# Reciprocal square roots of the norms as one GpSimd power instruction, in a two-block transformer kernel on one core

## The chip, the cores and the metric

The kernel runs on one core of a Trainium2 chip. The metric is the device time of one execution in microseconds (us). Engine names are those of the profile: PE is TensorE's matmul, PEld its weight load, DVE is VectorE, ACT is ScalarE, POOL is GpSimd, SP is SyncE, which here only issues DMAs.

## The reference

Two different transformer blocks of two layers each run one after the other on 256 tokens of width 1024, in float32. Every sublayer is wrapped in RMS norms, and the heads of the second block have norms of their own:

```python
def rmsnorm(x, g):
    y = x * lax.rsqrt(jnp.mean(x * x, -1, keepdims=True) + EPS)      # EPS = 1e-6
    return y * g

# first block, layer 0: gated delta rule and mLSTM; layer 1: windowed attention
h = h + rmsnorm(mix, gains[1])
hn = rmsnorm(h, gains[2])
ff = jnp.square(jax.nn.relu(hn @ w_up[layer])) @ w_down[layer]
h = h + rmsnorm(ff, gains[3])
h = h + jax.nn.sigmoid(h @ w_ple_gate[layer]) * (p[layer] @ w_ple[layer])

# second block, each layer: five groups of four heads (latent attention, forgetting attention, block
# attention, differential attention, memory attention), with norms over each head of q and k
xn = rmsnorm(x, attn_norm[l]);  x = x + concat(five groups of xn @ w_in[l]) @ w_o[l]
xn = rmsnorm(x, ffn_norm[l]);   x = x + (silu(conv(xn @ w_gate)) * (xn @ w_up)) @ w_down
```

## The kernel before, in words

Tokens lie on the 128 partitions in two token tiles, `t = 0` and `t = 1`, so that a norm of a row of 1024 is one column `[128, 1]` for each token tile, and the head norms of one tile are 3 to 16 columns. Weights come in blocks of 1 MB into two `raw` buffers; ACT (or DVE) rounds each into a high part `hi`, DVE takes the rest as a low part `lo`, and every product is three matmuls (high by high, low by high, high by low). The transposed activations stand in `aTh` and `aTl`. All instructions are written down by a `Recorder`, which then puts them into an order of its own: each engine gets, of what can start first, the instruction with the longest way to go, by rough prices in ns (`price`) and latencies between engines (`LAG`). All instructions are issued from one line (L571), so the profile is read by tiles: `s` are small tiles of up to 32 columns (the norms' scalars), `w` work tiles, `ps` PSUM banks, `gb` gains, `h` the residual stream.

A reciprocal square root is `rsqrt_of`: a guess from the bits on DVE (an int32 instruction), then a cubic and a quadratic step. For one column these are six further instructions, each of which goes to POOL or DVE (`rec.scalar`), whichever the planner finds free; for several columns they are ten instructions on POOL. The users are:

- `normed_T` (start of the program and, through `to_ff2`, ahead of each feed-forward of the second block): the row's factor is needed before the rows are transposed, so that PE waits for it.
- `residual` in `pre_ff1` and in `post` (first block): `h += y * r`, and the next transposes wait for `h`.
- `scaled_T`: the transposes take the rows without their factor; `r[t]` is multiplied in later, when banks are read.
- `headnorm`, `foxqk`, `group0` and `differential` in `mixers2` (second block): DVE multiplies the heads by their factors, and most of these products read a PSUM bank, which is free only then.
- `delta_out` (first block's layer 0), two columns each.

Where an input went in without its row's factor `r`, the norm that follows multiplies `r` in: `rsq(ms, w, r)` and `residual(..., pre)` work out `r * (r*r*ms + EPS) ** -0.5`.

Of the kernel before, what the change touches and what calls it, by code (L numbers as in the profile page):

```python
# [10 lines left out]
F32 = mybir.dt.float32  # L11
# [25 lines left out]
# ---------------------------------------------------------------- layout of small inputs  # L37
# [35 lines left out]
# ---------------------------------------------------------------- constants of the shapes  # L73
# [66 lines left out]
def layout(x):  # L140
# [126 lines left out]
class Recorder:  # L267
    """Takes the program's instructions down in the order in which it names them, and issues them in another:
    each engine gets, of what can start first, the instruction with the longest way to go. Every order of two
    instructions on overlapping data is kept, and a pool's tile is taken ahead of its turn only if the  # L270
    program's own order still fits into the pool from there on."""
# [12 lines left out]
    # ---------------------------------------------------------------- taking down  # L284
# [24 lines left out]
    def copy(self, out, src, scale=1.0):  # L309
        """out = scale * src on ScalarE or VectorE"""  # L310
# [67 lines left out]
    def price(self, op, out, ins):  # L378
        """a rough time in ns"""
# [66 lines left out]
    def swap(self, op):  # L446
        """the other form of an instruction"""
# [6 lines left out]
    def arrange(self):  # L454
# [33 lines left out]
        p0, gone, out = 0, [False] * n, []  # L488
        by_rank, top = sorted(range(n), key=lambda i: -ops[i].rank), 0
        while len(out) < n:  # L490
# [4 lines left out]
            for e, cand in avail.items():  # L495
                pick = None
                for i in cand:
# [9 lines left out]
                    for t in op.tiles:  # L507
                        if t not in taken:
                            p = pool[t]
                            room = self.pools[p] - (KEEP.get(p, 0) if op.rank < lead - SLACKTIME else 0)  # L510
                            if first[t] > p0 and use[p][p0 : first[t]].max() >= room:
# [62 lines left out]
class Loom:  # L574
    """Chains of dependent steps, each taken as far as what it needs is there."""
# [36 lines left out]
    def until(self, ready, *keys):  # L612
        """within a chain: wait for keys in ready"""
# [5 lines left out]
def program(ctx, tc, A, out, dbg=None):  # L619
# [64 lines left out]
    # ------------------------------------------------------------ resident data  # L684
# [51 lines left out]
    def whole(name, i, k, w):  # L736
        """block i of a packed weight as it is, for float32 products: four passes, but nothing to prepare"""
# [22 lines left out]
    def nmm(banks, a, hi, lo, first, last, n=512):  # L760
        """banks (column halves of n) += act^T @ W for one k-tile"""
# [1320 lines left out]
```

## Time and profile before

| | before |
|---|---|
| median of 3 runs | 1451.15 us (1449.95 to 1454.01) |
| span of the profiled execution, first to last instruction | 1450.2 us |
| TensorE busy | 1401.3 us |
| GpSimd busy | 199.9 us, 607 instructions |
| VectorE busy | 1000.2 us, 2320 instructions |

The profiled execution is known by its span alone; the median of the runs stands 0.9 us above it. Busy is the time in which an engine worked on at least one instruction.

### The profile page before, as it was taken

The page shows a single profiled execution, that of the slowest core. Times are in us where ns is not written, and L with a number is a line of the kernel's source. Part 1 is how long each engine was busy: PE and PEld are TensorE (multiplying, and loading weights), DVE is VectorE, ACT ScalarE, POOL GpSimd, SP SyncE. Part 2 cuts the span into 40 slices and gives each one's busy share as a digit, 9 for nine tenths or more (in the row PEclk, how much of TensorE's full clock was granted, in tenths as well). Part 3 has the DMA queues.
Part 4 walks back from the last instruction along what each step waited for, and adds up shares of the span by engine and source line. Part 5 has one row for each costly group of instructions (what it writes and reads, how often), then busy time and mean ns, then how long its engine had stood idle before and what let it go on. Part 6 is the DMA issues. An engine that isn't in the chain of part 4 may idle for free.

```text
span 1450.2 us, 23721 instructions
## 1 busy us (share of the span) xinstructions
PE 1401.3 (97%) x8856; PEld 1239.8 (85%) x8868; DVE 1000.2 (69%) x2320; ACT 796.1 (55%) x1810; POOL 199.9 (14%) x607
## 2 busy tenths in 40 slices
PE   7999999999999989999998999999999999999998
PEld 6899879999788879998786788999997778799997
DVE  6986776555778666556888766676567685656664
ACT  5554555444556635445575875564447586455543
POOL 0000530000110130000136412000004631100000
PEclk9999999999999999999999999999999999999999
DMA  8521344554553444545454222555544421345553
GB/s 331 190 88 59 116 172 166 209 193 177 208 191 126 158 160 166 212 175 213 146 206 170 108 103 88 204 203 180 198 157 174 149 103 59 118 166 182 184 196 115
DMA packets 36116, 236.40 MB, mean 163 GB/s; under 512 B 4128, under 2 KB 4384, under 8 KB 9888
## 3 DMA queue, kind: packets, MB, share of 16 engines
q1 hardware_dynamic: 36000, 234.88, 44.6%
q8 instruction: 70, 1.15, 0.3%
q14 instruction: 46, 0.38, 0.1%
HBM read 233.81 MB, written 1.05 MB: 162 GB/s over the span
## 4 chain that ended last, share of the span: by engine, by line
PE 76%; DVE 9%; POOL 9%; ACT 4%; issue 2%; DMA 0%; ACTq 0%; POOLq 0%; DVEq 0%
PE ps L571 76%; POOL s L571 9%; ACT w L571 3%; DVE w L571 3%; DVE s L571 2%; DVE lo L571 2%; DVE h L571 1%; DVE aTl L571 0%; DMA h<-in_x 0%; ACT hi L571 0%; ACT L571 0%; DVE tab L571 0%; ACT aTh L571 0%; ACT s L571 0%; DVE hi L571 0%
## 5 line engine op out<-in xcount | busy, mean ns | idle before, releaser
L571 ACT ACTIVATE hi<-raw 128x512 fp32r<-128x512 f32 (+1 forms) x789 | 436.7, 622 | 289.2 <-PE ps L571 241.6
L571 DVE TENSOR_TENSOR lo<-raw,hi 128x512 fp32r<-128x512 f32 (+2 forms) x836 | 522.2, 679 | 86.6 <-ACT hi L571 79.5
L571 PE MATMUL ps<-hi,w 128*128 128x512 f32 (+1 forms) x1272 | 390.6, 401 | 0.8 <-ACT w L571 0.6
L571 PE MATMUL ps<-aTh,hi 128*128 128x256 f32 x1256 | 327.6, 281 | 0.2 <-ACT aTh L571 0.2
L571 PE MATMUL ps<-aTh,lo 128*128 128x256 f32 x1256 | 323.7, 281 | 1.3 <-DVE lo L571 1.3
L571 PE MATMUL ps<-aTl,hi 128*128 128x256 f32 x1256 | 323.8, 281 | 0.7 <-DVE aTl L571 0.7
L571 PEld LDWEIGHTS ps<-hi,w 128*128 128x128 f32 x1272 | 222.0, 188 | 35.5 <-issue 1.9
L571 PEld LDWEIGHTS ps<-aTh,hi 128*128 128x128 f32 x1256 | 229.3, 189 | 11.1 <-ACT aTh L571 1.1
L571 PEld LDWEIGHTS ps<-aTh,lo 128*128 128x128 f32 x1256 | 227.7, 189 | 10.5 <-DVE lo L571 1.5
L571 PEld LDWEIGHTS ps<-aTl,hi 128*128 128x128 f32 x1256 | 226.9, 189 | 8.7 <-DVE aTl L571 1.0
L571 ACT ACTIVATE w<-ps 128x512 f32<-128x512 f32 (+4 forms) x260 | 131.3, 536 | 139.8 <-PE ps L571 133.4
L571 PE MATMUL ps<-lo,w 128*128 128x512 f32 (+1 forms) x620 | 202.6, 394 | 0.0
L571 PE MATMUL ps<-hi,aTh 128*128 128x512 f32 (+2 forms) x480 | 164.1, 373 | 4.1 <-DVE w L571 3.0
L571 PE MATMUL ps<-lo,aTh 128*128 128x512 f32 (+2 forms) x480 | 163.2, 370 | 4.9 <-DVE lo L571 4.9
L571 PE MATMUL ps<-hi,aTl 128*128 128x512 f32 (+2 forms) x480 | 162.8, 370 | 0.4 <-DVE aTl L571 0.3
L571 PE MATMUL ps<-w,w 128*128 128x128 f32 (+5 forms) x992 | 156.0, 286 | 1.3 <-DVE w L571 0.6
L571 POOL TENSOR_SCALAR s<-s 128x1 f32<-128x1 f32 (+6 forms) x222 | 78.2, 353 | 551.7 <-DVE s L571 294.0
L571 PEld LDWEIGHTS ps<-w,w 128*128 128x128 f32 (+1 forms) x992 | 139.2, 191 | 14.5 <-ACT w L571 2.7
L571 PE MATMUL ps<-cf,w 128*128 128x128 f32 (+1 forms) x612 | 115.3, 285 | 28.4 <-DVE w L571 23.6
L571 ACT ACTIVATE w<-w 128x512 fp32r<-128x512 f32 (+5 forms) x146 | 77.4, 538 | 109.4 <-DVE w L571 106.8
L571 PEld LDWEIGHTS ps<-cf,w 128*128 128x128 f32 (+1 forms) x612 | 81.8, 150 | 50.4 <-issue 18.5
L571 DVE CAST hi<-raw 128x512 fp32r<-128x512 f32 (+1 forms) x47 | 20.0, 425 | 151.5 <-PE ps L571 151.5
(101 smaller groups left out, 1348.6 us busy)
## 6 DMA issues: line engine op xcount, KB each, us to landing
raw<-in_wu SPq DMA_DIRECT2D x32, 1024.0 KB, 4.8
raw<-in_wd SPq DMA_DIRECT2D x32, 1024.0 KB, 5.4
raw<-in_fg SPq DMA_DIRECT2D x22, 1024.0 KB, 4.8
raw<-in_fu SPq DMA_DIRECT2D x22, 1024.0 KB, 4.8
raw<-in_fd SPq DMA_DIRECT2D x22, 1024.0 KB, 4.9
raw<-in_wi SPq DMA_DIRECT2D x20, 1024.0 KB, 4.8
raw<-in_w0t SPq DMA_DIRECT2D x10, 1024.0 KB, 4.8
raw<-in_wo SPq DMA_DIRECT2D x10, 1024.0 KB, 4.8
```

Source lines behind the costliest of these rows:

```text
L571: getattr(self.engines[op.eng], op.call)(*op.args, **op.kwargs)
```

## The change

Each reciprocal square root is one GpSimd instruction, `tensor_tensor` with the power operation and a constant tile of -0.5 (`root`). The rescaling by `RS` is gone with the polynomial; it remains in `rsqrt_rows`, the former polynomial on DVE, which one norm of 256 columns still uses. Where rows went in without their factor, the factor is no longer multiplied in: since `r = x ** -0.5`, `r * (r*r*ms + EPS) ** -0.5` equals `(ms + EPS * x) ** -0.5`, so the row brings its own eps (`row_eps`; after the squared feed-forward `EPS * x * x`). In `pre_ff1` the factor itself is then not needed at all, and no root is taken there. The planner has a price for the power, 300 ns and 165 ns for each column. Its search has a cache (`crowded`) that gives the same answers. Comments and docstrings are blanked, so that line numbers shift (L571 is L593).

```diff
         if op.eng == "pool":
+            if op.kwargs.get("op") == OP.pow:
+                return 300 + 165 * n
...
-    def rsqrt_of(x, w, eng, buf=None):
-        new = (lambda: small(w)[: x.shape[0]]) if buf is None else (lambda: buf()[: x.shape[0], :w])
-        z, t, q, xn = new(), new(), new(), new()
-        scalar = rec.scalar if w == 1 else eng.tensor_scalar
         dve.tensor_scalar(z.bitcast(I32), x.bitcast(I32), -0.5, 1597463007.0, op0=OP.mult, op1=OP.add)
-        scalar(xn, x, -1.0, None, op0=OP.mult)
...
+    nhalf = cpool.tile([P, 16], F32, name="nhalf")
+    pool.memset(nhalf, -0.5)
...
+    def root(x, w=1):
+        o = small(w)
+        pool.tensor_tensor(o, x, nhalf[:, :w], op=OP.pow)
+        return o
+
+    def rsq(ms, w=1, eps=None):
         x = small(w)
-        if r is None:
-            dve.tensor_scalar(x, ms, RS, RS * EPS, op0=OP.mult, op1=OP.add)
-            return rsqrt_of(x, w, pool)
-        r2 = small(1)
-        rec.scalar(r2, r, r, RS, op0=OP.mult, op1=OP.mult)
-        dve.tensor_scalar(x, ms, r2, RS * EPS, op0=OP.mult, op1=OP.add)
-        o = small(w)
-        rec.scalar(o, rsqrt_of(x, w, pool), r, None, op0=OP.mult)
-        return o
+        rec.scalar(x, ms, EPS if eps is None else eps, None, op0=OP.add)
+        return root(x, w)
...
+    def rms(srcs, both=True):
         a, b = meansq(srcs, D)
         x = small(1)
-        rec.scalar(x, a, b, RS * EPS, op0=OP.add, op1=OP.add)
-        return rsqrt_of(x, 1, pool)
+        rec.scalar(x, a, b, EPS, op0=OP.add, op1=OP.add)
+        return root(x) if both else None, x
+
+    def row_eps(x, n=1):
+        e = small(1)
+        if n == 1:
+            rec.scalar(e, x, EPS, None, op0=OP.mult)
+        else:
+            rec.scalar(e, x, x, EPS, op0=OP.mult, op1=OP.mult)
+        return e
...
-    def residual(t, banks, g, pre=None):
+    def residual(t, banks, g, eps=EPS):
...
-        if pre is None:
-            rec.scalar(x, a, b, RS * EPS, op0=OP.add, op1=OP.add)
-            r = rsqrt_of(x, 1, pool)
-        else:
-            p2, s, r = small(1), small(1), small(1)
-            rec.scalar(p2, pre, pre, None, op0=OP.mult)
-            rec.scalar(s, a, b, p2, op0=OP.add, op1=OP.mult)
-            rec.scalar(x, s, RS * EPS, None, op0=OP.add)
-            rec.scalar(r, rsqrt_of(x, 1, pool), pre, None, op0=OP.mult)
+        rec.scalar(x, a, b, eps, op0=OP.add, op1=OP.add)
+        r = root(x)
...
-        yield from scaled_T(t, g2, r)
+        yield from scaled_T(t, g2, None, e, 2)
...
-            residual(t, down[t], g3, pre=r2)
+            residual(t, down[t], g3, e[t])
...
-            headnorm(fold(bank, 8), y, 8, 64, r[t])
+            headnorm(fold(bank, 8), y, 8, 64, e[t])
```

The change leaves POOL 140 rows of 612 (counting constants and branches), among them 64 powers: 24 of one column, 8 of two, 4 of three, 12 of four, 8 of eight, 4 of twelve and 4 of sixteen. DVE has 2154 instructions instead of 2322. The SP queue has the same DMAs, with three neighbouring ones exchanged. All of this changes the planner's order; here are the places on which most rests.

On POOL, among the head norms of the second block's first layer, these rows work out one root of 16 columns (`s_1632` is the mean square with eps, `s_1635` the root; the rows of 12 columns belong to another). Before:

```order
L571 TENSOR_SCALAR s_1638<-s_1632 128x16
L571 TENSOR_TENSOR s_1593<-s_1599,s_1593 128x12
L571 TENSOR_TENSOR s_1636<-s_1635 128x16
L571 TENSOR_TENSOR s_1636<-s_1636,s_1632 128x16
L571 TENSOR_SCALAR s_1639<-s_1636 128x16
L571 TENSOR_TENSOR s_1637<-s_1639,s_1636 128x16
L571 TENSOR_SCALAR s_1640<-s_1637 128x16
L571 TENSOR_TENSOR s_1635<-s_1640,s_1635 128x16
L571 TENSOR_TENSOR s_1636<-s_1635 128x16
L571 TENSOR_TENSOR s_1636<-s_1636,s_1638 128x16
L571 TENSOR_SCALAR s_1641<-s_1636 128x16
L571 TENSOR_TENSOR s_1635<-s_1641,s_1635 128x16
```

Now, at the same place (`s_1277` and `s_1289` are the rows' eps):

```order
L593 TENSOR_SCALAR s_1441<-s_1438 128x12
L593 TENSOR_TENSOR s_1442<-s_1441,nhalf 128x12
L593 TENSOR_SCALAR s_1475<-s_1474,s_1277 128x16
L593 TENSOR_TENSOR s_1476<-s_1475,nhalf 128x16
L593 TENSOR_SCALAR s_1504<-s_1503,s_1289 128x16
L593 TENSOR_TENSOR s_1505<-s_1504,nhalf 128x16
```

Eleven dependent rows for each root have become two, an addition and the power.

On DVE, the start of the program (`h_81` and `h_82` are the token tiles, `s_90` and `s_102` their factors, `gb_85` the gain). Before:

```order
L571 TENSOR_SCALAR s_91<-s_90,s_93 128x1
L571 TENSOR_SCALAR s_101<-s_98 128x1
L571 TENSOR_SCALAR s_90<-s_91,s_90 128x1
L571 TENSOR_SCALAR s_102<-s_101 128x1
L571 TENSOR_SCALAR s_105<-s_101 128x1
L571 SCALAR_TENSOR_TENSOR w_94<-h_81,s_90,gb_85 128x512
L571 SCALAR_TENSOR_TENSOR w_95<-h_81,s_90,gb_85 128x512
L571 TENSOR_SCALAR s_103<-s_102,s_105 128x1
L571 TENSOR_SCALAR s_102<-s_103,s_102 128x1
L571 SCALAR_TENSOR_TENSOR w_106<-h_82,s_102,gb_85 128x512
L571 SCALAR_TENSOR_TENSOR w_107<-h_82,s_102,gb_85 128x512
```

Now:

```order
L593 TENSOR_SCALAR s_90<-s_87 128x1
L593 TENSOR_SCALAR s_99<-s_96 128x1
L593 SCALAR_TENSOR_TENSOR w_92<-h_81,s_91,gb_86 128x512
L593 SCALAR_TENSOR_TENSOR w_93<-h_81,s_91,gb_86 128x512
L593 SCALAR_TENSOR_TENSOR w_101<-h_82,s_100,gb_86 128x512
L593 SCALAR_TENSOR_TENSOR w_102<-h_82,s_100,gb_86 128x512
```

Both tiles' products now follow each other with nothing between them.

On DVE, `pre_ff1` of the first block's second layer, where rows with `gb` and `ps` are the second tile's bias and those with `w` and `gb` the gain. Before:

```order
L571 TENSOR_TENSOR w_1113<-ps_1075,gb_1086 128x512
L571 TENSOR_TENSOR w_1114<-ps_1076,gb_1086 128x512
L571 TENSOR_TENSOR w_1118<-w_1113,gb_1087 128x512
L571 TENSOR_TENSOR w_1119<-w_1114,gb_1087 128x512
L571 SCALAR_TENSOR_TENSOR h_81<-w_1094,s_1097,h_81 128x512
L571 TENSOR_SCALAR s_1121<-s_1120 128x1
L571 SCALAR_TENSOR_TENSOR h_81<-w_1095,s_1097,h_81 128x512
L571 TENSOR_SCALAR s_1123<-s_1122 128x1
L571 TENSOR_TENSOR w_1101<-h_81,gb_1088 128x512
L571 TENSOR_SCALAR s_1122<-s_1121,s_1124 128x1
L571 TENSOR_TENSOR w_1102<-h_81,gb_1088 128x512
```

Now:

```order
L593 TENSOR_TENSOR w_1022<-ps_990,gb_1001 128x512
L593 SCALAR_TENSOR_TENSOR h_81<-w_1009,s_1012,h_81 128x512
L593 TENSOR_TENSOR w_1023<-ps_991,gb_1001 128x512
L593 TENSOR_TENSOR w_1027<-w_1022,gb_1002 128x512
L593 TENSOR_TENSOR w_1013<-h_81,gb_1003 128x512
L593 SCALAR_TENSOR_TENSOR h_81<-w_1010,s_1012,h_81 128x512
L593 TENSOR_TENSOR w_1028<-w_1023,gb_1002 128x512
L593 SCALAR_TENSOR_TENSOR h_82<-w_1027,s_1030,h_82 128x512
L593 TENSOR_TENSOR w_1014<-h_81,gb_1003 128x512
```

The small steps are gone, and the first tile's row for the transposes (`w_1013`, before `w_1101`) stands four wide rows after the second tile's first bias instead of six.

## Rows read from the trace of the kernel before

**Rows 1.** The page, span and busy times: us (share of the span) and instructions.

```profile
span 1450.2 us, 23721 instructions
PE 1401.3 (97%) x8856; PEld 1239.8 (85%) x8868; DVE 1000.2 (69%) x2320; ACT 796.1 (55%) x1810; POOL 199.9 (14%) x607
```

**Rows 2.** The page, chain that ended last: share of the span by engine.

```profile
PE 76%; DVE 9%; POOL 9%; ACT 4%; issue 2%; DMA 0%; ACTq 0%; POOLq 0%; DVEq 0%
```

**Rows 3.** Stretches at norms: length, busy PE, PEld, DVE, ACT, POOL, clock, DMA share.

```profile
150.00:200.00 50.00, 49.32 (x241) 39.45 (x241) 37.16 (x105) 25.88 (x63) 28.38 (x88) 1.00 0.39 137
...
196.00:206.00 10.00, 9.03 (x36) 5.19 (x35) 8.86 (x21) 8.68 (x21) 4.33 (x10) 1.00 0.34 124
386.00:397.00 11.00, 10.16 (x40) 5.94 (x38) 9.40 (x23) 7.74 (x17) 5.92 (x10) 1.00 0.37 127
...
700.00:708.00 8.00, 5.74 (x36) 4.21 (x34) 7.51 (x16) 7.55 (x17) 2.19 (x6) 1.00 0.19 67
741.00:818.00 77.00, 69.29 (x321) 55.15 (x320) 60.47 (x212) 49.28 (x109) 47.24 (x158) 0.98 0.46 166
...
893.00:903.00 10.00, 9.21 (x52) 7.34 (x52) 8.71 (x18) 8.11 (x18) 4.78 (x10) 1.00 0.29 107
1104.00:1180.00 76.00, 67.88 (x323) 54.58 (x324) 56.74 (x187) 50.90 (x116) 43.23 (x161) 0.98 0.47 166
```

**Rows 4.** PE in order of time, the longest gaps: idle before in brackets.

```profile
516.13 2.13 PE L571 MATMUL ps<-cf,w 128*128 128x128 f32 x8 [5.99 <-DVE w L571]
...
793.57 0.79 PE L571 MATMUL ps<-lo,aTh 128*128 128x512 f32 x1 [2.65 <-DVE lo L571]
...
1144.38 0.41 PE L571 MATMUL ps<-cf,w 128*128 128x128 f32 x2 [2.77 <-DVE s L571]
...
1256.73 0.63 PE L571 MATMUL ps<-cf,w 128*128 128x128 f32 x4 [2.61 <-DVE w L571]
```

**Rows 5.** The five us behind those gaps, columns as in rows 3.

```profile
516.00:521.00 5.00, 4.73 (x22) 4.00 (x22) 4.67 (x9) 2.99 (x7) 2.94 (x6) 0.55 0.04 15
...
793.00:798.00 5.00, 4.43 (x15) 3.54 (x16) 4.12 (x12) 1.47 (x3) 2.52 (x8) 0.66 0.32 92
1144.00:1149.00 5.00, 4.62 (x18) 3.70 (x19) 4.45 (x23) 1.67 (x4) 2.54 (x10) 0.66 0.24 102
...
1256.00:1261.00 5.00, 3.79 (x17) 3.16 (x18) 4.36 (x10) 2.95 (x6) 2.64 (x5) 0.67 0.00 0
```

**Rows 6.** DVE's waits for POOL, at 741 to 818 and at 1104 to 1180: us, times, longest.

```profile
DVE w L571 <- POOL s L571: 10.4, 9, 2.4
...
DVE w L571 <- POOL s L571: 8.6, 6, 2.7
```

**Rows 7.** POOL's instructions by form: busy us, mean ns, idle before.

```profile
L571 POOL TENSOR_SCALAR s<-s,s 128x1 f32<-128x1 f32 x69 | 37.6, 546 | 449.3 <-DVE s L571 278.0 <-ACT w L571 167.6 <-ACT hi L571 0.7
...
L571 POOL TENSOR_TENSOR s<-s,s 128x4 f32<-128x4 f32 x60 | 14.5, 246 | 4.1
...
L571 POOL TENSOR_TENSOR s<-s,s 128x16 f32<-128x16 f32 x20 | 6.5, 325 | 1.2
```

**Rows 8.** Small tiles, DVE and POOL: ns shortest/median/longest, first and last start.

```profile
L571 DVE TENSOR_SCALAR s<-s x192: 135/163/216, 5.4 to 1257.9; 128x2 f32<-128x2 f32 x44, 128x1 f32<-128x1 f32 x42, 128x1 int32<-128x1 int32 x28, 128x4 f32<-128x4 f32 x24
...
L571 POOL TENSOR_TENSOR s<-s,s x200: 191/203/2006, 149.9 to 1221.6; 128x4 f32<-128x4 f32 x27, 128x8 f32<-128x8 f32 x21, 128x2 f32<-128x2 f32 x20, 128x16 f32<-128x16 f32 x12
```

**Rows 9.** The start, in order of time: start us, us, instruction.

```profile
5.42 0.46 DVE L571 TENSOR_SCALAR s<-s 128x1 f32<-128x1 f32 x3 [5.42 <-ACT w L571]
...
7.36 1.34 POOL L571 TENSOR_SCALAR s<-s,s 128x1 f32<-128x1 f32 x1 [5.43 <-DVE s L571]
...
10.02 1.42 DVE L571 SCALAR_TENSOR_TENSOR w<-h,s,gb 128x512 f32<-128x512 f32 x2
```

**Rows 10.** Before the second feed-forward, in order of time, columns as in rows 9.

```profile
1254.20 0.68 DVE L571 TENSOR_TENSOR h<-ps,h 128x512 f32<-128x512 f32 x1
...
1259.63 1.41 DVE L571 SCALAR_TENSOR_TENSOR w<-h,s,gb 128x512 f32<-128x512 f32 x2
```

More of the change, by code (lines that the diff above doesn't have):

```diff
@@ L488, in arrange, with crowded, moved @@
         p0, gone, out = 0, [False] * n, []
+        full = {}
+        def crowded(p, room):
+            k = full.get((p, room))
+            if k is None or k < p0:
+                v = use[p][p0:n] >= room
+                k = p0 + int(v.argmax())
+                if k < n and not v[k - p0]:
+                    k = n
+                full[p, room] = k
+            return k
+        def moved(p):
+            room = self.pools[p]
+            full.pop((p, room), None)
+            full.pop((p, room - KEEP.get(p, 0)), None)
         by_rank, top = sorted(range(n), key=lambda i: -ops[i].rank), 0
@@ L510, in arrange @@
                             room = self.pools[p] - (KEEP.get(p, 0) if op.rank < lead - SLACKTIME else 0)
-                            if first[t] > p0 and use[p][p0 : first[t]].max() >= room:
+                            if first[t] > p0 and crowded(p, room) < first[t]:
                                 ok = False
@@ L545, in arrange @@
                 p = pool[t]
+                if t not in taken or left[t] == 1:
+                    moved(p)
                 if t not in taken:
@@ L808, in program, with rsqrt_rows @@
     RS = 4.0 * (8.0 / 3.0) ** 6
-    def rsqrt_of(x, w, eng, buf=None):
-        new = (lambda: small(w)[: x.shape[0]]) if buf is None else (lambda: buf()[: x.shape[0], :w])
-        z, t, q, xn = new(), new(), new(), new()
-        scalar = rec.scalar if w == 1 else eng.tensor_scalar
+    def rsqrt_rows(x, w, buf):
+        z, t, q, xn = (buf()[: x.shape[0], :w] for _ in range(4))
         dve.tensor_scalar(z.bitcast(I32), x.bitcast(I32), -0.5, 1597463007.0, op0=OP.mult, op1=OP.add)
-        scalar(xn, x, -1.0, None, op0=OP.mult)
+        dve.tensor_scalar(xn, x, -1.0, None, op0=OP.mult)
@@ L900, in scaled_T @@
             to_aT(t, q, xs[q])
-        r[t] = rms(halves(h[t]))
+        rr, x = rms(halves(h[t]), r is not None)
+        if r is not None:
+            r[t] = rr
+        if e is not None:
+            e[t] = row_eps(x, n)
     def normed_T(t, g):
-        r = rms(halves(h[t]))
+        r, _ = rms(halves(h[t]))
         xs = [w2(), w2()]
@@ L1407, in mixer_c, with pre_ff1 @@
                lambda it, t: loom.join(("C", it[1], t)))
-    def pre_ff1(l, t, banks, g1, g2, r, bias=None):
+    def pre_ff1(l, t, banks, g1, g2, e, bias=None):
         if bias is not None:
@@ L1447, in early, with ff1 @@
                 put(u, t, b[:, 0:256])
-    def ff1(l, r, pw, end):
+    def ff1(l, e, pw, end):
         down = [[acc(), acc()], [acc(), acc()]]
@@ L1495, in post @@
         def post(t):
-            r2 = small(1)
-            dve.tensor_tensor(r2, r[t], r[t], op=OP.mult)
-            residual(t, down[t], g3, pre=r2)
+            residual(t, down[t], g3, e[t])
             yield
@@ L1522, in ff1, with headnorm @@
                lambda it, t: loom.join(("post", l, t)))
-    def headnorm(x, dst, nh, d, row=None):
+    def headnorm(x, dst, nh, d, eps=None):
         sq = fold(w2()[:, : nh * d], nh)
@@ L1530, in headnorm @@
         dve.tensor_reduce(ms, sq, axis=AX, op=OP.add)
-        r = rsq(ms, nh, row)
+        r = rsq(ms, nh, eps)
         dve.tensor_tensor(dst, x, bc(r, d), op=OP.mult)
@@ L1616, in rope_tables2, with mixers2 @@
         return tab, lam_t
-    def mixers2(l, r, mem, tab, lam, end):
+    def mixers2(l, r, e, mem, tab, lam, end):
         lam_init = 0.8 - 0.6 * math.exp(-0.3 * l)
@@ L1976, in out0 @@
             g2.append(gain(2))
-        loom.spawn(pre_ff1(0, t, banks, g1[0], g2[0], r), ("pre", 0, t))
+        loom.spawn(pre_ff1(0, t, banks, g1[0], g2[0], e), ("pre", 0, t))
     mixer_ab(out0)
@@ L1989, in into1 @@
             gc.append(gain(4))
-        yield from scaled_T(t, gc[0], rc)
-    ff1(0, r, per_layer_input(0), into1)
+        yield from scaled_T(t, gc[0], rc, None)
+    ff1(0, e, per_layer_input(0), into1)
     loom.drain()
     dumph("f0")
-    r = [None, None]
+    e = [None, None]
     g1, g2, gbo = [], [], []
@@ L2003, in out1 @@
             g2.append(gain(6))
-        loom.spawn(pre_ff1(1, t, banks, g1[0], g2[0], r, gbo[0]), ("pre", 1, t))
+        loom.spawn(pre_ff1(1, t, banks, g1[0], g2[0], e, gbo[0]), ("pre", 1, t))
     pw = per_layer_input(1)
@@ L2017, in into2 @@
             gi.append(gain(8))
-        yield from scaled_T(t, gi[0], ri)
-    ff1(1, r, pw, into2)
+        yield from scaled_T(t, gi[0], ri, ei)
+    ff1(1, e, pw, into2)
     mem = memory(0, *memory_T(0))
@@ L2054, in after @@
                     gi.append(gain(9))
-                yield from scaled_T(t, gi[0], ri)
+                yield from scaled_T(t, gi[0], ri, ei)
         if l == 0:
```

46 lines of the change are left out of this document (16 added, 30 removed).

## The prediction

> **What bounds the kernel now.** I read the page first, then the stretches in which TensorE is not full, then who waits there. TensorE is busy 1401.3 of 1450.2 us [rows 1]; its matmuls are the same before and after. So whatever the norms cost, the change can give back only TensorE's 48.9 us of idle time and what a lowered clock costs behind long gaps. The chain that ended last runs through PE for 76% and through POOL for 9%, about 125 us [rows 2]; that 9% is no measure of the gain, since TensorE mostly works on other blocks meanwhile. The idle time has to be read place by place.
>
> Six stretches at norms [rows 3]: PE idles 0.97 us of 10 at 196 (`pre_ff1`, layer 0), 0.84 of 11 at 386 (`post`, layer 0), 2.26 of 8 at 700 (`post`, layer 1), 0.79 of 10 at 893 (first `to_ff2`), and in the head norms of the second block 7.71 of 77 and 8.12 of 76. The reader should see in the same rows that POOL is busy 47.24 and 43.23 us in these two long stretches, and that DVE is at 60.47 and 56.74, ACT at 49.28 and 50.90: POOL's steps depend on one another, the others are near two thirds to four fifths full. Two more gaps stand by themselves [rows 4]: 5.99 us before 516.13 (`pre_ff1`, layer 1) and 2.61 us before 1256.73 (second `to_ff2`); 2.65 and 2.77 us are the longest of the head norms. Behind each of these four gaps the granted clock over five us is 0.55, 0.66, 0.66 and 0.67 [rows 5], a part of them at the level of 1.2 instead of 2.4 GHz: a loss of 2.25, 1.7, 1.7 and 1.65 us. In the long stretches DVE's head products wait for POOL 10.4 and 8.6 us in 15 waits [rows 6], more than TensorE's idle time there, so I take POOL's chains for its cause.
>
> **The power's price.** No row shows one. The nearest rows are POOL's instructions on small tiles: 246 ns for a product of four columns, 325 ns for sixteen, 546 ns for one column with two scalars [rows 7]. That is the low end, about 0.25 us whatever the width. The high end is all that it replaces: eleven steps on POOL of 0.25 to 0.33 us, some 3.2 us. In between stands the planner's price, 300 ns and 165 ns a column. I can test the planner's other prices: for a product of four columns it has 162 ns, and the shortest of POOL's products took 191 ns, the median 203 [rows 8]. The means are higher by 50 to 120 ns, and single instructions took up to 2.0 us, so something holds POOL up at times. The planner's prices thus lie near the shortest durations, and I take its price with a fifth on top: 0.5 to 0.75 us for one column, some 3 us for sixteen.
>
> The Trainium skill (GPSIMD Engine Reference, 4.1 Engine selection) says that elementwise work belongs on VectorE, GpSimd being about half as fast; the trace agrees, with 163 ns for a small DVE instruction against 203 [rows 8]. The same page (7. Performance pitfalls for Q7 kernels) puts a dependent float32 step at 4 cycles, which at its 1.2 GHz is an estimated 3.3 ns: 165 ns a column would be some 50 dependent steps, 150 steps would be 500 ns, and by that the sum below would become that of the second rival.
>
> **Part by part.**
>
> *Start.* Tile 0's sum is there at 5.42; the second tile's two products start at 10.02 and take 1.42 together, ending at 11.44 [rows 9]. All later products of the first blocks need both tiles. Now: addition 0.16, hand-over 0.1, power 0.55, so the first product starts near 6.25, and the new order has all four products in a row: 4 x 0.71 = 2.84, ending at 9.1. The second tile's power must be done at 7.7, which it is at this price. **-2.3 us.** With 3.2 us for a power, two of them in a row on POOL end at 12, and this is +2.
>
> *The four small stretches* have 4.86 us idle together. DVE is busy 7.5 to 9.4 us of each, and the four to ten small steps that it loses are 0.16 us each; its wide products stay. I take half: **-2.4** (0 to -4).
>
> *`pre_ff1`, layer 1.* After the second tile's bias can start, DVE's new order has five wide rows of 0.64 to 0.75 us up to the first tile's row for the transposes: 3.4 us, against 5.99 of gap. So the first transpose can gain 2.6, but the number of wide rows up to the last one is the same, and DVE, not POOL, is what is late next. **-1.8** (0 to -2.6); I let the clock's loss stand.
>
> *Second `to_ff2`.* The second tile's `h` is complete at 1254.88, and the last of four products ends at 1261.04 [rows 10]. In the new order four products (0.71 each), one low part (0.68) and one `aTl` (0.64) follow each other: 4.2 us, ending at 1259.0. **-2.0**, and the gap shrinks from 2.61 to some 1.6 us; whether the clock then falls no row tells, so I take 1.0 of the 1.65 us back: **-3.0** together (0 to -3.7).
>
> *Head norms.* Each layer has 16 roots with 118 columns in all (two each of 3, 12 and 16, six of 4, four of 8). Their POOL work falls from 47 and 43 us to 16 x 0.3 + 118 x 0.165 = 24.3 us, and a root alone from 3.2 us to between 0.8 us (3 columns) and 2.9 us (16 columns), so the wide ones gain little. DVE loses a share of 168 instructions of 0.16 us. Of 15.83 us idle I take half, since DVE and ACT become the next to be late: -8. The two gaps behind which the clock falls end in DVE's waits; if they shrink like the rest, 3 of 3.4 us come back. **-11** (0 to -19).
>
> The `mixer_ab` roots (two columns) lie beside matmuls, PE being busy 49.32 of 50 us there [rows 3]: nothing. The absent roots of `pre_ff1` and the eps products lie beside matmuls: nothing; what covers them is the first two blocks of `early`. The SP queue keeps its order but for three exchanges: nothing.
>
> Sum: 2.3 + 2.4 + 1.8 + 3.0 + 11.0 = 20.5 us off the profiled span of 1450.2, so 1429.7, and with the 0.9 us by which the median stands above the span **1430.6 us**. At the low end of the power's price all gaps named could nearly close, -29 us in all: 1422. At the high end only DVE's lost steps remain, some -3 us: 1448.
>
> **The rivals.** *First, DVE and ACT are the bound of the head norms anyway.* DVE is busy 79% there, and its wide products and low parts stay. For it: the gap before 793.57 ended in a low part, not in POOL. Then the head norms give 4 instead of 11, and the time is 1437.6. Against it: the 19 us in which DVE waits for POOL.
>
> *Second, slower: the power is dear by the column.* It must cost (45 - 4.8) / 118 = 0.34 us a column for POOL's work in the head norms to be what it was. At 0.5 us it is 63.8 us, 17 to 21 us more for each layer; TensorE is already 90% busy there and has nothing to fill it with: +36, less some 6 us from the other places, 1481. For it: no row excludes it. Against it: the planner's other prices fit.
>
> *Third, the first power is slow.* POOL's first step at 7.36 took 1.34 us [rows 9] where the mean of its kind is 0.55 [rows 7]; a stall of 0.8 us at the first power would stand in the start: 1431.4. The Trainium skill (GPSIMD Engine Reference, 2.1 Instruction dispatch) gives some 6 us for the first call of a freshly loaded GpSimd routine; by that 1436.6, and no row here shows such a load.
>
> *Fourth, it changes nothing.* The planner lays everything out anew, and waits appear elsewhere, as in the 2.65 us before 793.57, where a transfer and DVE's order met: 1450.
>
> **How the numbers follow.** Forecast, 1424 to 1437: 0.55. All gaps close, 1422 or less: 0.07. First rival: 0.17. Third: 0.06. Fourth: 0.06. Second: 0.09. A measurement of this kernel tells 0.3%, 4.4 us, from no change. Faster by more: 0.55 + 0.07 + 0.17 + 0.06 = 0.85; within it 0.06; slower 0.09. The range runs from below the closed gaps, 1417, to 1446, short of the high end of the price; that leaves out the second and the fourth rival and some of the edges.
>
> **What would show it.** Powers of about 0.5 to 0.75 us for one column and near 3 us for sixteen; POOL busy about 100 instead of 199.9 us; PE idle of some 4 us in each head-norm stretch; the second tile's products at the start ending near 9 us; a gap of some 3.4 us in `pre_ff1`, layer 1, still with a lowered clock, and one under 2 us before the last feed-forward with a full clock. Wrong would be: powers over 0.34 us a column, or DVE's waits for POOL as long as before.

## The result, and the profile after

The changed kernel takes 1461.3 us in the median (1460.7 to 1465.8) against 1451.1 for the kernel before: a ratio of 1.0073, 95% interval 1.0053 to 1.0093. It is slower by 0.7%, where 1430.6 was forecast.

The page of the changed kernel, span and busy times, answers to [rows 1], and the chain that ended last to [rows 2]:

```profile
span 1459.8 us, 23054 instructions
...
PE 1419.7 (97%) x8858; PEld 1258.2 (86%) x8868; DVE 981.4 (67%) x2152; ACT 789.5 (54%) x1799; POOL 105.2 (7%) x135
...
PE 90%; ACT 4%; DVE 3%; issue 1%; DMA 1%; POOL 1%; POOLq 0%; ACTq 0%
```

GpSimd left the chain (9% to 1%), and TensorE's idle time fell from 48.9 to 40.1 us. But TensorE's busy time rose by 18.4 us, for the same matmuls. The three largest groups of matmuls of 256 columns (busy us, mean ns of one), before and then now:

```profile
L571 PE MATMUL ps<-aTh,hi 128*128 128x256 f32 x1256 | 327.6, 281 | 0.2 <-ACT aTh L571 0.2
L571 PE MATMUL ps<-aTl,hi 128*128 128x256 f32 x1256 | 323.8, 281 | 0.7 <-DVE aTl L571 0.7
L571 PE MATMUL ps<-aTh,lo 128*128 128x256 f32 x1256 | 323.7, 281 | 1.3 <-DVE lo L571 1.3
```

```profile
L593 PE MATMUL ps<-aTh,hi 128*128 128x256 f32 x1256 | 333.2, 286 | 0.5 <-DVE aTl L593 0.5
L593 PE MATMUL ps<-aTh,lo 128*128 128x256 f32 x1256 | 328.9, 285 | 1.6 <-DVE lo L593 1.6
L593 PE MATMUL ps<-aTl,hi 128*128 128x256 f32 x1256 | 327.8, 284 | 0.3 <-DVE aTl L593 0.3
```

These matmuls overlap, each starting long before the one ahead of it has ended, so the spacing of their starts tells more than the duration of one. Where they follow each other less than 160 ns apart, their starts lie 115.8 ns apart before and 118.7 after (mean of 3,171 and 3,138 pairs). The two ranges do not meet in any part of the run: by pieces of 200 us they are 115.0 to 116.8 and 118.4 to 119.1. These 3,768 matmuls by 2.9 ns are 11 us, and the 960 of 512 columns with `aTh` and `aTl` (229.4 to 232.4 ns) another 3.

The powers, POOL's instructions by form, cost what was forecast:

```profile
L593 POOL TENSOR_TENSOR s<-s,nhalf 128x1 f32<-128x1 f32 x24 | 16.3, 680 | 461.9 <-DVE s L593 460.8
...
L593 POOL TENSOR_TENSOR s<-s,nhalf 128x8 f32<-128x8 f32 x8 | 14.2, 1779 | 7.5 <-DVE s L593 7.1
...
L593 POOL TENSOR_TENSOR s<-s,nhalf 128x16 f32<-128x16 f32 x4 | 12.0, 3006 | 0.3
```

And DVE's waits for them ahead of its wide products, over the whole run, are 8.9 us where they were 28.7:

```profile
DVE w L593 <- POOL s L593: 8.9, 12, 1.8
```

The stretches that answer to [rows 3, 5]: the head norms (744 to 821 and 1109 to 1185), the ends of the two mixers (828 and 1194, 14 us each; a mixer is the attention part of a layer of the second block), and the places behind `pre_ff1` of layer 1 (516) and the second `to_ff2` (1261); columns as there:

```profile
744.00:821.00 77.00, 76.29 (x378) 62.41 (x378) 66.35 (x220) 56.05 (x137) 27.85 (x21) 1.00 0.49 174
828.00:842.00 14.00, 10.91 (x55) 8.85 (x54) 7.44 (x20) 6.86 (x25) 0.00 (x0) 0.80 0.42 152
1109.00:1185.00 76.00, 73.57 (x362) 60.05 (x364) 61.54 (x181) 55.90 (x134) 25.20 (x19) 1.00 0.50 180
1194.00:1208.00 14.00, 10.91 (x51) 8.48 (x50) 7.29 (x19) 9.38 (x34) 0.00 (x0) 0.77 0.45 151
516.00:521.00 5.00, 3.49 (x14) 2.86 (x15) 4.24 (x8) 3.89 (x11) 3.63 (x4) 0.50 0.63 210
1261.00:1271.00 10.00, 7.63 (x43) 6.47 (x42) 8.60 (x15) 7.44 (x17) 2.28 (x3) 0.83 0.00 0
```

The head norms idle 0.71 and 2.43 us where they idled 7.71 and 8.12. The end of each mixer now idles 3.09 us at a clock of 0.80 and 0.77, with POOL at rest (0.00), so that no power is under way there. PE in order of time there, to be held against [rows 4]:

```profile
833.99 0.66 PE L593 MATMUL ps<-cf,w 128*128 128x128 f32 x4 [1.56 <-DVE w L593]
835.39 0.66 PE L593 MATMUL ps<-cf,w 128*128 128x128 f32 x4 [0.75 <-ACT w L593]
836.74 1.54 PE L593 MATMUL ps<-w,w 128*128 128x64 f32 x6 [0.69 <-ACT w L593]
```

Four transposes, four transposes, value products: one attention, with nothing else to fill its waits. So there are two questions: why matmuls became slower, and why idle time came back.

### The profile page after: what moved, and what is told of

Its sections match the earlier page's. It is cut to its first block, busy times and chain, and to the rows that moved or that the text cites. A ratio compares the mean times of both kernels' runs of the same rounds, so it can differ in the third digit from the quotient of the medians.

```text
span 1459.8 us, 23054 instructions
## 1 busy us (share of the span) xinstructions
PE 1419.7 (97%) x8858; PEld 1258.2 (86%) x8868; DVE 981.4 (67%) x2152; ACT 789.5 (54%) x1799; POOL 105.2 (7%) x135
## 4 chain that ended last, share of the span: by engine, by line
PE 90%; ACT 4%; DVE 3%; issue 1%; DMA 1%; POOL 1%; POOLq 0%; ACTq 0%
PE ps L593 90%; ACT w L593 3%; DVE w L593 2%; ACT hi L593 1%; POOL s L593 1%; DVE lo L593 1%; DVE s L593 1%; DMA raw<-in_fd 0%; DVE h L593 0%; DMA h<-in_x 0%; DVE aTl L593 0%; ACT L593 0%; ACT aTh L593 0%; POOLq L2091 0%; ACT s L593 0%
## 5 line engine op out<-in xcount | busy, mean ns | idle before, releaser
L593 ACT ACTIVATE hi<-raw 128x512 fp32r<-128x512 f32 (+1 forms) x781 | 429.4, 619 | 314.8 <-PE ps L593 273.4
L593 DVE TENSOR_TENSOR lo<-raw,hi 128x512 fp32r<-128x512 f32 (+2 forms) x836 | 520.8, 680 | 89.9 <-ACT hi L593 75.7
L593 PE MATMUL ps<-hi,w 128*128 128x512 f32 x1272 | 388.2, 401 | 0.4 <-ACT hi L593 0.4
L593 PE MATMUL ps<-aTh,hi 128*128 128x256 f32 x1256 | 333.2, 286 | 0.5 <-DVE aTl L593 0.5
L593 PE MATMUL ps<-aTh,lo 128*128 128x256 f32 x1256 | 328.9, 285 | 1.6 <-DVE lo L593 1.6
L593 PE MATMUL ps<-aTl,hi 128*128 128x256 f32 x1256 | 327.8, 284 | 0.3 <-DVE aTl L593 0.3
L593 PEld LDWEIGHTS ps<-hi,w 128*128 128x128 f32 x1272 | 222.3, 188 | 33.3 <-issue 1.1
L593 PEld LDWEIGHTS ps<-aTh,hi 128*128 128x128 f32 x1256 | 231.2, 190 | 12.2 <-DVE aTl L593 0.8
L593 PEld LDWEIGHTS ps<-aTh,lo 128*128 128x128 f32 x1256 | 228.8, 190 | 12.4 <-DVE lo L593 2.0
L593 PEld LDWEIGHTS ps<-aTl,hi 128*128 128x128 f32 x1256 | 228.5, 190 | 8.1 <-DVE aTl L593 0.9
L593 ACT ACTIVATE w<-ps 128x512 f32<-128x512 f32 (+4 forms) x260 | 129.0, 517 | 139.6 <-PE ps L593 130.6
L593 PE MATMUL ps<-lo,w 128*128 128x512 f32 (+1 forms) x620 | 199.3, 394 | 0.0
L593 PE MATMUL ps<-hi,aTh 128*128 128x512 f32 (+2 forms) x480 | 164.1, 374 | 3.5 <-ACT aTh L593 1.8
L593 PE MATMUL ps<-lo,aTh 128*128 128x512 f32 (+2 forms) x480 | 163.8, 370 | 0.1
L593 PE MATMUL ps<-w,w 128*128 128x128 f32 (+4 forms) x992 | 160.2, 293 | 2.5 <-ACT w L593 2.2
L593 PE MATMUL ps<-hi,aTl 128*128 128x512 f32 (+2 forms) x480 | 162.3, 369 | 0.0
L593 PEld LDWEIGHTS ps<-w,w 128*128 128x128 f32 (+1 forms) x992 | 145.6, 196 | 16.6 <-ACT w L593 3.7
L593 PE MATMUL ps<-cf,w 128*128 128x128 f32 (+1 forms) x612 | 116.5, 287 | 25.4 <-DVE w L593 20.8
L593 DVE CAST hi<-raw 128x512 fp32r<-128x512 f32 x55 | 23.5, 427 | 172.6 <-PE ps L593 172.6
L593 ACT ACTIVATE w<-w 128x512 fp32r<-128x512 f32 (+5 forms) x145 | 76.0, 533 | 115.7 <-DVE w L593 113.0
L593 PEld LDWEIGHTS ps<-lo,w 128*128 128x128 f32 x620 | 110.1, 188 | 16.1
L593 POOL TENSOR_TENSOR s<-s,nhalf 128x1 f32<-128x1 f32 (+6 forms) x64 | 76.8, 1203 | 645.5 <-DVE s L593 641.0
```

The lines of the kernel that those rows point to most:

```text
L593: getattr(self.engines[op.eng], op.call)(*op.args, **op.kwargs)
```

## Experiments

"Before" in every comparison is the kernel before on the same chip (1451.0 to 1452.3 us).

**Placement alone.** The constant `nhalf` is 64 bytes of each partition, and every tile that is laid out after it moves up by as much. e1 and e4 are the kernel before with an unused tile in that place, of 64 and 384 bytes; e2 and e3 are the changed kernel with `nhalf` made 128 and 384 bytes wide.

```diff
     cols = cpool.tile([P, NCOLS], F32, name="cols")
...
+    spare = cpool.tile([P, 16], F32, name="spare")
+    pool.memset(spare[:, 0:16], -0.5)
```

e1, 64 bytes. 

> The kernel before with one unused constant tile of 16 columns (64 bytes a partition) at the place where the change puts its constant, so that the weight and work tiles stand 64 bytes further, as in the changed kernel; norms and order as before. Theory A (the shift slows the matmuls of 256 columns from 116 to 119 ns): 1463 us, between 1460 and 1466, with a spacing near 119 ns. Theory B (the new order and the waits at the norms): 1451 us and 116 ns.

e2, 128 bytes. 

> The changed kernel with its constant tile twice as wide, so that the weight and work tiles stand 128 bytes further than before instead of 64; norms and order as in the changed kernel. Theory A: the matmul spacing is back at 116 ns and the time is 1447 us (1444 to 1450). Theory B: 1461 us, as the changed kernel.

e3, 384 bytes. 

> The changed kernel with its constant tile 384 bytes wide, so that the weight and work tiles start at a multiple of 2048 bytes. Theory A, if 128 bytes are what counts: 1447 us, as the kernel with 128 bytes; if larger multiples help further, below 1444. Theory B: 1461 us.

e4, 384 bytes. 

> The kernel before with an unused tile of 384 bytes at that place, so that its weight and work tiles start at a multiple of 2048 bytes. Theory A, if 128 bytes are what counts: 1451 us; if larger multiples help further, below 1448. Theory B: 1451 us.

Measured: e1 1463.9 us (1.0085, 1.0072 to 1.0098), e2 1458.1 (1.0041, 1.0026 to 1.0055), e3 1457.2 (1.0036, 1.0024 to 1.0049), e4 1455.4 (1.0028, 1.0017 to 1.0039). e1 has every instruction of the kernel before in the same order on every engine, and one memset more; it is slower by as much as the changed kernel, with matmuls of 283 ns, 118.6 ns apart. Theory A holds; the idea that a multiple of 128 bytes would be as good as before does not.

**The change with every other tile in its old place.** e5 has the changed kernel's instructions in their order, and puts `nhalf` into a pool behind all others:

```diff
+    endp = ctx.enter_context(tc.tile_pool(name="endp", bufs=1))
...
-    nhalf = cpool.tile([P, 16], F32, name="nhalf")
+    nhalf = endp.tile([P, 16], F32, name="nhalf")
```

> The changed kernel with its constant of -0.5 in a pool of its own behind all others, so that every other tile stands where the kernel before has it; instructions and order are the changed kernel's own. Theory A (the 64-byte shift of the tiles cost the time, the change itself gives back idle time): spacing of the 256-column matmuls back at 116.0 ns, PE busy near 1402 us, and 1461.3 less about 12.7 = 1449 us, level with before within 0.4%. Theory B (the new order and its waits cost the time): 1459 to 1462 us, slower than before by over 0.5%. In both the gaps at the ends of the mixers (three together near 3.0 us) stay, since the order is the same.

Measured: 1450.3 us, 0.9983 (0.9971 to 0.9995); matmuls 115.7 ns apart again. The whole slowdown is the placement. TensorE's busy time is 1406.7 us, not the 1402 that were expected: 13.0 of the 18.4 us came with the placement and are gone, the other 5.4 stay, with every tile in its old place. And the change itself then gives 0.2%, next to nothing, so the second question remains.

**The old order with the power in it.** e6 is e5, with the order not planned but taken from the kernel before: a table gives each instruction its place and engine there, and a power stands where the chain's first step stood. In the traces TensorE, ScalarE and SyncE then have the same instructions in the same order as before.

```diff
+            kind, n = op.key
+            if kind == "p":
+                p, e = at["p"][n], names[at["pe"][n]]
+            elif kind == "x":
+                p, e = at["x"][n], names[at["xe"][n]]
+            elif kind == "root":
+                p, e = at["c"][n], "pool"
```

> As e5, but TensorE, ScalarE and SyncE get exactly the kernel before's sequence of instructions, and VectorE and GpSimd theirs with each norm's chain replaced by the one power. Theory A with C (the planner's new layout gave back elsewhere what the power saved): the head-norm gaps shrink as in the changed kernel, 7 to 8 us of idle time less in those two stretches and the clock behind them, and no new gaps at the mixers' ends: 1436 to 1444 us. Theory D (the power saves little by itself; idle time moved because the program was laid out anew): 1447 to 1452 us, the head-norm gaps still there.

Measured: **1420.6 us, 0.9785 (0.9768 to 0.9802)**: 30 us faster than before, and than e5. Its page, and then the two mixers from end to end (last write of `h` to last write of `h`), of the kernel before, of e5 and of e6:

```profile
span 1418.8 us, 23046 instructions
...
PE 1391.2 (98%) x8856; PEld 1239.2 (87%) x8868; DVE 979.3 (69%) x2166; ACT 794.0 (56%) x1810; POOL 90.9 (6%) x110
```

```profile
731.42:898.30 166.88, 157.68 (x864) 131.33 (x866) 121.65 (x393) 112.46 (x306) 64.62 (x206) 0.99 0.37 135
...
1093.10:1254.20 161.10, 152.55 (x843) 127.71 (x845) 112.80 (x340) 107.87 (x297) 57.17 (x203) 0.99 0.35 122
```

```profile
729.70:893.92 164.22, 158.76 (x859) 133.31 (x861) 117.77 (x355) 109.43 (x301) 35.30 (x36) 0.98 0.40 143
...
1090.76:1254.65 163.89, 158.06 (x852) 133.39 (x854) 111.50 (x313) 107.20 (x294) 30.67 (x27) 0.97 0.35 127
```

```profile
724.96:880.52 155.56, 153.47 (x856) 130.09 (x858) 117.14 (x358) 111.73 (x306) 32.56 (x29) 1.00 0.40 145
...
1074.90:1223.57 148.67, 148.56 (x841) 126.97 (x844) 109.37 (x315) 106.93 (x296) 29.18 (x22) 1.00 0.38 132
```

The mixers take 167 and 161 us before, 164 and 164 in e5, 156 and 149 in e6. In e6 TensorE idles 2.1 and 0.1 us of them at a clock of 1.00. The 14 us in which e5's mixers run thin, 94 and 95 us behind their start, and then 14 us of e6 at a like distance (96 and 87):

```profile
824.00:838.00 14.00, 10.91 (x55) 8.59 (x54) 7.86 (x21) 7.99 (x28) 0.00 (x0) 0.83 0.44 152
...
1186.00:1200.00 14.00, 10.91 (x49) 8.53 (x48) 6.55 (x18) 8.85 (x32) 0.00 (x0) 0.71 0.42 151
```

```profile
821.00:835.00 14.00, 13.71 (x97) 12.12 (x96) 10.27 (x32) 14.00 (x52) 0.00 (x0) 1.00 0.37 133
...
1162.00:1176.00 14.00, 13.95 (x89) 11.97 (x89) 11.87 (x35) 13.74 (x53) 0.00 (x0) 1.00 0.24 77
```

In e6 these hold 97 and 89 matmuls with ACT busy 14.00 and 13.74 us, in e5 55 and 49, and there no engine is full. PE in order of time, e5 and then e6:

```profile
827.50 0.39 PE L593 MATMUL ps<-hi,aTl 128*128 128x512 f32 x1
827.74 0.38 PE L593 MATMUL ps<-cf,w 128*128 128x128 f32 x2
829.68 0.66 PE L593 MATMUL ps<-cf,w 128*128 128x128 f32 x4 [1.56 <-DVE w L593]
831.08 0.66 PE L593 MATMUL ps<-cf,w 128*128 128x128 f32 x4 [0.75 <-ACT w L593]
832.42 2.87 PE L593 MATMUL ps<-w,w 128*128 128x64 f32 x16 [0.69 <-ACT w L593]
```

```profile
829.28 0.60 PE L636 MATMUL ps<-w,w 128*128 128x256 f32 x2
829.72 0.82 PE L636 MATMUL ps<-cf,w 128*128 128x128 f32 x6
830.37 0.56 PE L636 MATMUL ps<-w,w 128*128 128x64 f32 x4
830.77 0.39 PE L636 MATMUL ps<-cf,w 128*128 128x128 f32 x2
```

The last matmul of the projections (`ps<-hi,aTl`) starts at 827.50 in e5, and from 827.74 on one attention stands alone; in e6 scores (256 columns), transposes (`cf`) and value products (64 columns) of several alternate without a gap. The head norms by themselves, the same matmuls as in the two long stretches of [rows 3], in e6:

```profile
734.40:801.80 67.40, 66.28 (x321) 54.64 (x319) 60.39 (x200) 48.41 (x109) 25.40 (x15) 1.00 0.53 188
1086.00:1151.10 65.10, 65.10 (x325) 53.72 (x326) 54.93 (x170) 50.37 (x115) 23.85 (x14) 1.00 0.50 178
```

They take 67.4 and 65.1 us instead of 77 and 76, and TensorE idles 1.1 of them instead of 15.8. Theory C holds, and more strongly than I had put it (1436 to 1444).

**Is it the planner's price?** e7 gives the planner the measured price of a power, e9 one as dear as the old chain, both with `nhalf` at the end; e8 is the kernel before with one number of the planner moved by 5%. (First lines of the diff: e7; in e9 it is `2000 + 150 * n`. Last lines: e8.)

```diff
-                return 300 + 165 * n
+                return 515 + 155 * n
...
-SLACKTIME = 4e4
+SLACKTIME = 3.8e4
```

e7. 

> As e5, with the planner's price of a power set to what the profile of the changed kernel shows (515 + 155 ns for each column instead of 300 + 165), so that the layout knows the late ends. If the new gaps come from a layout planned with too cheap powers: 1440 to 1446 us, 4 us or more below e5. If the layout is a lottery within a few us: within 4 us of e5 on either side.

e8. 

> The kernel before with one number of the planner moved by 5% (how far ahead it may take a tile out of turn: 38 instead of 40 us) and nothing else; every tile in its place, norms as before. It shows what a new layout alone does: if layouts are worth the same, 1449 to 1453 us; if the layout of the kernel before is a lucky one (theory C), 1454 to 1462 us.

e9. 

> As e5 (constant at the end, the planner's own layout), with the planner told that a power takes 2000 + 150 ns for each column, about what the old chain of steps was priced at, so that it plans the norms as early as it did before while they end early. Theory E (the layout was worse because cheap norms were planned with no slack, and any lateness reached TensorE): 1420 to 1432 us, near e6. Theory F (the kernel before's order is one lucky layout among many, and a price does not bring it back): 1440 to 1452 us, like e5 and e7.

Measured: e7 1445.5 us (0.9957, 0.9942 to 0.9972), e8 1452.9 (1.0015, 1.0002 to 1.0027), e9 1451.9 (1.0012, 0.9999 to 1.0026). Theory E falls as a whole, and still explains a part. With e9's dear price the mixers take 158 and 157 us, less than in e5; but what they gain is lost elsewhere. e7 lies in the range expected of too cheap powers, 4.9 us below e5, but that is a sixth of the 30 us. e8 lies in the range for layouts that are worth the same: a new layout of the old program costs 2 us, not 30. That speaks against theory F, a lucky old order, though F's range holds e9's time and one other layout is little to go by. From 80 to 120 us of e9, then of e6:

```profile
80.00:120.00 40.00, 32.32 (x235) 29.80 (x234) 30.72 (x108) 19.52 (x33) 0.00 (x0) 0.91 0.25 85
```

```profile
80.00:120.00 40.00, 40.00 (x317) 38.18 (x316) 33.39 (x127) 20.93 (x39) 0.00 (x0) 1.00 0.31 106
```

TensorE idles 7.7 of 40 us in e9 where POOL does nothing at all, so no power stands there. In e7 it is 6.3, in e5 0.1, and in the kernel before 0.0. (The profiled execution of e9 took 1458.2 us, the longest of its twelve, so it tells the place better than the amount.) The planner's layouts of the changed program (1445.5, 1450.3, 1451.9) each lose some 25 to 31 us against the old order, in different places.

**Do the two costs add up?** e10 is e6 with `nhalf` where the changed kernel has it.

```diff
-    nhalf = endp.tile([P, 16], F32, name="nhalf")
+    nhalf = cpool.tile([P, 16], F32, name="nhalf")
```

> As e6 (the kernel before's order with the power in the place of each chain), but the constant stands where the changed kernel has it, so that the later tiles are shifted by 64 bytes. If placement and order are two costs that add up: 1420.6 + 11 to 13 = 1432 to 1434 us, spacing of the 256-column matmuls 118.7 ns. If the shift only matters together with the changed kernel's layout: 1419 to 1424 us.

Measured: 1432.9 us (0.9875, 0.9862 to 0.9887), 12.3 above e6, with the matmuls 118.6 ns apart and PE busy 1404.9 instead of 1391.2 us in the same sequence of matmuls. They add up.

**Which tiles, and which offsets?** Tiles are laid out in the order `aTh`, `aTl`, some small tables, `raw`, `hi`, `lo`, `w`, `gb`, `s`. e11 and e12 are the kernel before with the 64 unused bytes behind `raw` (the diff) and behind `lo`, again with every instruction in its order. e13 to e18 are e6 with other offsets: in e13 `nhalf` is the first tile of all; in the others a tile behind `raw` has 64, 256, 8, 48 and 56 columns of 4 bytes (e14 to e18; it is `nhalf` itself but for e16).

```diff
     rawp = ctx.enter_context(tc.tile_pool(name="rawp", bufs=NRAW))
+    gapp = ctx.enter_context(tc.tile_pool(name="gapp", bufs=1))
     hlp = ctx.enter_context(tc.tile_pool(name="hlp", bufs=NHL))
...
+    spare = gapp.tile([P, 16], F32, name="spare")
```

e11. 

> The kernel before with 64 unused bytes between raw and hi: hi, lo, w, gb and s are shifted, raw is not. If the shift of the tiles that the matmuls read (hi, lo) costs the time: spacing 118.7 ns and 1461 to 1465 us, as in e1. If it is raw's place (what the DMA writes, ScalarE and VectorE read): spacing 116.0 ns and 1450 to 1452 us.

e12. 

> The kernel before with 64 unused bytes between lo and w: w, gb and s are shifted, raw, hi and lo are not. If hi and lo are what matters: spacing 116.0 ns and 1450 to 1452 us. If it is w (what ScalarE and VectorE write while TensorE reads): spacing 118.7 ns and 1461 to 1465 us.

e13. 

> As e6, but the constant is the first tile of all, so that every tile is shifted by 64 bytes, aTh and aTl (the moving operands) as well as hi and lo (the weights); their distances stay as in the kernel before. Theory G (the distance of the weights from the moving operand matters): spacing 116 ns and 1419 to 1423 us, like e6. Theory H (the weights' own address matters): spacing 118.7 ns and 1431 to 1434 us, like e10.

e14. 

> As e6, with the constant in 256 bytes between raw and hi: hi, lo, w, gb and s are shifted by 256. If only the remainder by 128 or 256 bytes matters: 116 ns and 1419 to 1423 us. If every shift tried so far is worse than none, as 128 and 384 were: about 117.4 ns and 1425 to 1429 us.

e15. 

> As e14 with 1024 bytes. If the pattern repeats within 1024 bytes: 116 ns and 1419 to 1423 us; if not, 117 to 119 ns and 1425 to 1434 us.

e16. 

> As e6, with 32 unused bytes between raw and hi (the constant stays at the end). If the cost grows with the distance from the next multiple of 128 bytes: 117 to 118 ns and 1425 to 1430 us; if any place off a multiple of 64 or 128 bytes costs the same: 118.7 ns and 1431 to 1434 us; if only odd multiples of 64 are bad: 116 ns and 1419 to 1423 us.

e17. 

> As e14 with 192 bytes: the distance from aTh to hi becomes a multiple of 256 bytes (it is 64 more than one in the kernel before and in e13, e14 and e15, which were fast; 96 and 128 more in e16 and e10, which were slow; 192 more in e2 and e3, which lay between). If the remainder of the distance by 256 decides and small remainders are good: 1417 to 1422 us. If 64 is a favoured remainder by itself: 1425 to 1434 us.

e18. 

> As e14 with 224 bytes: the distance is 32 more than a multiple of 256. If the remainder of the distance by 256 decides and small remainders are good: 1417 to 1422 us. If a place that is off a multiple of 64 bytes costs by itself, as in e16: 1430 to 1434 us.

Measured, by what is left when the distance from `aTh` to `hi` is divided by 256 bytes (`lo` and `aTl` lie whole multiples of 256 further on). The distance counts two small tables of 16 and 4 bytes as 32 bytes each, which no run shows; were it otherwise, all rests would be off by the same amount, and their differences are those of the edits:

| rest | kernels with the order of e6 | kernels with the order of before or after |
|---|---|---|
| 0 | e17 1431.6 | |
| 32 | e18 1427.4 | |
| 64 | e6 1420.6, e13 1420.7, e14 1419.6, e15 1420.4 | before 1451.1, e5 1450.3, e12 1453.3 |
| 96 | e16 1432.3 | |
| 128 | e10 1432.9 | after 1461.3, e1 1463.9, e11 1462.1 |
| 192 | | e2 1458.1, e3 1457.2, e4 1455.4 |

Intervals of the ratios to before are some 0.0015 to either side. The rows of the group `ps<-aTh,hi` in e10, and in e13, where all tiles are shifted by the same 64 bytes but `aTh` with them:

```profile
L636 PE MATMUL ps<-aTh,hi 128*128 128x256 f32 x1256 | 330.8, 284 | 0.2 <-ACT aTh L636 0.2
```

```profile
L636 PE MATMUL ps<-aTh,hi 128*128 128x256 f32 x1256 | 327.5, 281 | 0.0
```

So it is neither `raw` (e11) nor the address of the weights, but their distance from the moving operand: theory G. e12's 2 us fit it too, for there `w` moved away from `hi` and `lo`, with which it is multiplied elsewhere. Its largest group with `w`, before and then in e12:

```profile
L571 PE MATMUL ps<-hi,w 128*128 128x512 f32 x1256 | 386.5, 402 | 0.8 <-ACT w L571 0.6 <-DVE w L571 0.2
L571 PE MATMUL ps<-hi,w 128*128 128x512 f32 x1256 | 389.8, 404 | 0.7 <-ACT w L571 0.5 <-DVE w L571 0.2
```

The starts of the matmuls of `hi` or `lo` with `w` lie 232.6 ns apart in e12 (1,313 pairs under 300 ns) and between 229.1 and 229.7 in every other run. The matmuls of 256 columns, whose operands did not move in e12, are 114.9 ns apart there, 0.9 less than before; why is open. A shift by 256 or 1024 bytes changes nothing, and of the six rests tried 64 is the best, by 7 to 12 us in the order of e6 and by 4 to 8 us over 192 in the other orders. That small rests would be good, as e17's and e18's text had it, is wrong; e18 lies in neither of its two ranges. e14 is the fastest of all, 0.9779 (0.9763 to 0.9795), not to be told from e6.

## Why the prediction was wrong

**The step that failed first** is in the opening part: "its matmuls are the same before and after. So whatever the norms cost, the change can give back only TensorE's 48.9 us of idle time and what a lowered clock costs". They were the same in number, not in duration. The line `nhalf = cpool.tile(...)` stood in the diff, and the sum has no term for its place. It cost 11 to 13 us (after against e5, e10 against e6, e1 against before), and it alone decided the sign. No rival had it: the only one on the slower side, with 0.09, was a dear power, and the power was not dear.

**The second** is the sum's silent assumption that the changed program keeps the order of the one before except where a norm stands. The fourth rival, "The planner lays everything out anew, and waits appear elsewhere ... 1450", had 0.06; e5, the change without the shift, takes 1450.3. Its mechanism, waits elsewhere in a new layout, is what e5 and e6 show, though not at the wait before 793.57 that I named as an example. That its figure fits is luck: 1450 stood for no change, and 1450.3 is 30 us given by the power and as much taken by the new order.

**The mechanism itself was right and its size too small.** In the old order and places the power gives 30.4 us where the sum was 20.5, and the term that was mis-sized is the head norms. TensorE has the same sequence in e6 as before, so the same weight load can be found in both traces, and how much earlier it starts in e6, behind a place less ahead of it, is what that place gave. The places below come to 30.7 of the 31.4 us by which the two spans differ.
- Price of the power: 680 ns for one column (taken: 500 to 750), 3006 for sixteen (some 3000); POOL busy 105.2 us (about 100). The second rival, a dear power, is out. (The 163 against 203 ns that I read as agreeing with a GpSimd half as fast are a quarter apart, and of two different instructions.)
- Head norms: 9.6 and 10.9 us, where 11 was summed for both. "Of 15.83 us idle I take half, since DVE and ACT become the next to be late" is the step: they were not late. In e6 14.7 of the 15.8 us of idle time closed, DVE's waits for powers ahead of its wide products are 0.2 us in the whole run, and TensorE's busy time fell by 5.8 us for the same matmuls, 3.4 of it the lowered clock of [rows 5] (1.7 and 1.7 us), as the clock is 1.00 in both stretches of e6. So the first rival is out in the old order.
- The four small stretches: 1.3, 1.8, 0.6 and 1.3 us, 5.0 where half of 4.86 was summed. Here too nearly all came.
- `mixer_ab`: 1.8 us between 150 and 195, where nothing was summed.
- `pre_ff1`, layer 1: 1.8 us, as summed; the gap is 4.33 us in e6 instead of 5.99. In the changed kernel it is 2.91 and 0.69, with the clock at 0.50.
- Second `to_ff2`: 1.6 of the 3.0 us. The gap is 2.14 us in e6 instead of 2.61, 1.53, 0.23 and 0.56 in the changed kernel, and the clock fell in both.
- Start, up to 30 us: 0.0 of 2.3 us in e6, because the products there wait for a transfer of `gb`, start at 8.48 and end at 11.22, against 11.44; the sum had no such wait. In e13, e14 and e15, with the same order, it is 1.0, 2.8 and 1.2. In the changed kernel the second power begins at 7.47 us and takes 1.00, and the four products start at 7.31 and end at 10.05. The first power takes 0.55 us at 6.29, so the third rival is out. The Trainium skill (GPSIMD Engine Reference, 2.1 Instruction dispatch) has some 6 us for the first call of a freshly loaded routine; no run here shows one.

**What stays open.** Why the planner's layouts of the changed program are some 25 to 31 us behind the old order. The runs show where the time goes (the thin ends of the mixers in e5, 80 to 120 us in e7 and e9), and that neither price mends it; which of the planner's rules brings it about was not tried. Open too is why just a rest of 64 is good.

## What to carry to other kernels

A new small constant is also a shift of all that is laid out behind it. Put it last, or compare the spacing of the largest groups of matmuls before and after ahead of any other explanation: equal counts with longer busy time at the same clock is not a wait. The spacing tells it more clearly than the mean duration, which is 282 to 283 ns in e5 with every tile in its old place, where the kernel before has 281. And where a planner lays a program out as a whole, a cheaper step is two changes at once; replay the old order with the new step in it to tell them apart, and keep that order if it is the better one (1420.6 against 1450.3 us here).

## What was unexpected of the hardware

The spacing of float32r matmuls with 128 stationary and 256 moving columns depends on the distance in SBUF between the two operands: 115.7 to 116.2 ns at a rest of 64 bytes by 256 (e6, e13, e14, e15), 117.2 and 117.3 at 192 (e2, e3, e4), 118.4 to 118.7 at 32, 96 and 128 (e18, e16, e10), 119.3 at 0 (e17), and over the run that is up to 12 us of 1420. Which rest is best differs with the form: the matmuls of 512 columns with `aTh` and `aTl` are 229.4 to 230.2 ns apart at 64, 232.4 and 232.5 at 128, 233.1 to 233.4 at 32, 96 and 192, and 228.1 at 0, where those of 256 are slowest. e12 shows it for a second pair of operands, `hi` or `lo` with `w`: 229.4 to 232.6 ns. That the distance is not all, e12 shows too: its pairs of 256 columns, at the distance of before, are 114.9 ns apart. The Trainium skill (TensorE: Matmul & The Clock Gate, Step-by-step: what each phase is for) says that weights and moving operand are read through ports of their own, so that loading the next weights takes nothing from the running matmul. The runs show that the two are not wholly independent: with the same sequence, only their distance changed, TensorE's busy time goes from 1391.2 and 1392.0 us (e6 and e13) to 1404.9 (e10). That the two reads collide in the memory would fit, and is argued, not shown.
